# Second feed-forward projection with seven block products instead of eight, on 16 of its 22 blocks

## The chip, the cores and the metric

One core of a Trainium2 chip runs the whole kernel in one launch. The metric is the time of one execution on the device, in microseconds (us); lower is better. All inputs and the output lie in the chip's main memory as float32.

## The reference, cut to what matters

The reference is a stack of two layers with mixed attention and then two layers with a mixer and a convolutional feed-forward network (FFN). The change touches only the FFN, which runs twice (once in each of the last two layers), on S = 512 rows, a model width of 1024 and D_FF = 2816 inner units:

```python
def conv_ffn(x, w_up, conv_w, conv_b, w_down):
    a, g = jnp.split(x @ w_up, 2, axis=-1)
    g = lax.conv_general_dilated(g, conv_w[:, None, :].astype(g.dtype), window_strides=(1,),
                                 padding=((CONV_W - 1, 0),), dimension_numbers=('NWC', 'WIO', 'NWC'),
                                 feature_group_count=D_FF) + conv_b
    return (jax.nn.gelu(g) * a) @ w_down
...
    x = layer_norm(alpha * x + y, ln_g[l, 0], ln_b[l, 0])
    y = conv_ffn(x, ffn_w_up[l], ffn_conv_w[l], ffn_conv_b[l], ffn_w_down[l])
    x = layer_norm(alpha * x + y, ln_g[l, 1], ln_b[l, 1])
```

The second projection is a product of a 512 x 2816 matrix, gelu(g) * a, with w_down, 2816 x 1024. The inner units are cut into 22 blocks of 128.

## The kernel before, in words

**Numbers in two parts.** Each float32 operand of a large product is split into a rounded part `hi` (a cast on ACT) and a rest `lo` (a subtraction on DVE), and each product is three matmuls: hi·hi, hi·lo and lo·hi. `split` does this for activations, `load_w` for a weight tile: SP loads 128 x 512 float32 (256 KB) into one of four `raw` buffers (line 213), ACT writes `w[:, 0]` (line 226) and DVE writes `w[:, 1]` (line 227). `mm3` (lines 231 to 233) and `fsteps` (lines 1060 to 1062) issue the three matmuls. A weight tile `w` takes one of a set of slots, in turn: six that are always there (`NW`) and more that a stage adds with `more_w`. A slot comes free when the last matmul that reads it has run.

**The FFN (`ffn`, line 1467).** The hidden state stands transposed in `hT` (8 blocks of 128 x 512). The inner units are taken in three parts of 8, 7 and 7 blocks. In each part, groups of up to four blocks go through the first projection: eight weight tiles for `g`, and for each block j a pass of 8 steps of three matmuls (24 matmuls) into one PSUM bank, which `ev_g` reads (convolution on ACT and DVE, gelu on ACT); then eight weight tiles for `a`, with `ev_a`, which multiplies (line 1497) and splits the result into an `act` tile (lines 1499 and 1500). Then comes the second projection of the part: for each half n of the 1024 columns and each tile t of 128 rows, `down_part` runs one pass over the blocks of the part, three matmuls for each (`dsteps` and `mm3`), and adds the PSUM bank to `z[t]` on DVE (line 1532). With 8 blocks a part has 16 weight tiles, 8 passes of 24 matmuls and 8 additions to `z`. In the last part the layer norm follows each row tile (`ln_apply`), and in the first FFN the next layer's first loads are woven in.

The first group of an FFN runs in two halves of the rows (lines 1517 to 1519), since the last rows of `hT` come late. The FFN adds 7 slots for weight tiles to the 6 there are. Convolution weights are loaded into the tile `cwr` (lines 1475 and 1476), turned by TensorE (line 1506).

**What sets the order.** The program is unrolled. A scheduler fixes each engine's order when the kernel is built, from its own estimate of when each operand is ready; every engine and each DMA queue then runs its list in order and waits by semaphores. All DMAs are issued by SP. POOL (GpSimd) does small work only, in the FFN only the reciprocal root of the layer norm (lines 281 and 282). PSUM has eight banks: four for `mm`, two for `t` (transposes) and two for `o`, which the FFN doesn't use.

Of the kernel before, what the change touches and what calls it, by code (L numbers as in the profile page):

```python
# [9 lines left out]
F32 = mybir.dt.float32  # L10
F32R = mybir.dt.float32r
# [3 lines left out]
OP = mybir.AluOpType  # L15
# [5 lines left out]
S = 512  # L21
# [100 lines left out]
def _body(ctx, tc, nc, a, out, stop):  # L122
    V, SC, GP, PE = nc.vector, nc.scalar, nc.gpsimd, nc.tensor
# [30 lines left out]
    def ps_mm():  # L154
        return psum("mm", [128, 512], 4)
# [6 lines left out]
    def ps_o():  # L162
        return psum("o", [128, 512], 2)
# [34 lines left out]
    yT = hp.tile([128, 2, 4, S], F32R, name="yT")  # L198

    wslots = [(wp, NW)] * NW  # L200
    wturn = [0]

    def more_w(name, n, stack, side):
        pl = pool(name, stack=stack, side=side)
        wslots.extend([(pl, n)] * n)
        stack.callback(lambda: wslots.__delitem__(slice(len(wslots) - n, None)))
# [34 lines left out]
    def split(hi, lo, ps, scale=None):  # L241
        if scale is None:
            SC.copy(hi, ps)  # L243
            V.tensor_tensor(lo, ps, hi.bitcast(F32), op=OP.subtract)
        else:
            SC.activation(hi, ps, AF.Copy, scale=scale)
            V.scalar_tensor_tensor(lo, ps, scale, hi.bitcast(F32), op0=OP.mult, op1=OP.subtract)
# [64 lines left out]
    def tick():  # L312
        clock[0] += 1
        for p in [p for p in pend if p[0] <= clock[0]]:
            pend.remove(p)
            p[1]()
# [731 lines left out]
    R2 = math.sqrt(2.0)  # L1048
# [418 lines left out]
    def ffn(l, zst, z, rows, opf, est):  # L1467
        halves = (slice(0, 256), slice(256, 512))[::-1 if l else 1]
        fst = ExitStack()
        drain(opf)  # L1470
        est.close()
        fp = pool(f"ff{l}", stack=fst, side="left")
        more_w(f"wf{l}", 7, fst, "left")
        cwr = fp.tile([88, 128], F32, name="cwr")
        nc.sync.dma_start(cwr[0:66], a["ffn_conv_w_2"][l].rearrange("i (c p) -> (i c) p", p=128))
        nc.sync.dma_start(cwr[66:88], a["ffn_conv_b_2"][l].rearrange("(c p) -> c p", p=128))
        cw = fp.tile([128, 4, 22], F32, name="cw")
        up, down = a["ffn_w_up_2"][l], a["ffn_w_down_2"][l]
        c0 = 0
        st6 = {}  # L1480
        for part, nch in enumerate((8, 7, 7)):
            act = [fp.tile([128, 2, S], F32R, name="act", bufs=10) for _ in range(nch)]
            for q0 in range(0, nch, 4):
                nq = min(4, nch - q0)
                ge = {}

                def ev_g(j, ps):
                    c = c0 + q0 + j
                    g0 = fp.tile([128, S], F32, name="g0", bufs=2)
                    SC.activation(g0, ps, AF.Identity, scale=cw[:, 2, c:c + 1], bias=cw[:, 3, c:c + 1])  # L1490
                    V.scalar_tensor_tensor(g0[:, 1:], ps[:, :S - 1], cw[:, 1, c:c + 1], g0[:, 1:], op0=OP.mult, op1=OP.add)  # L1491
                    V.scalar_tensor_tensor(g0[:, 2:], ps[:, :S - 2], cw[:, 0, c:c + 1], g0[:, 2:], op0=OP.mult, op1=OP.add)
                    ge[j] = fp.tile([128, S], F32, name="ge", bufs=6)
                    SC.activation(ge[j], g0, AF.Gelu_apprx_tanh)

                def ev_a(j, ps):
                    V.tensor_tensor(ge[j], ge[j], ps, op=OP.mult)  # L1497
                    d = act[q0 + j]
                    SC.copy(d[:, 0], ge[j])
                    V.tensor_tensor(d[:, 1], ge[j], d[:, 0].bitcast(F32), op=OP.subtract)  # L1500

                ws = load_ws(up, FF + 128 * (c0 + q0), 128 * nq, K8)
# [45 lines left out]
                if m:  # L1548
                    save_x(t, z[t])

            if part == 2:
                lg = rows(1)
            w = [{k: load_w(down, 128 * (c0 + k), 512 * n, 512) for k in range(nch)} for n in range(2)]
            for t in (3, 2, 1, 0):
                down_part(0, w[0], t)
# [472 lines left out]
    zst, z, rows = z0[0]  # L2028
# [9 lines left out]
    zst, z, rows, opf, mst = odd_mixer()  # L2038
# [37 lines left out]
```

## Time and profile before

| | us |
|---|---|
| median of 3 runs | 1965.36 |
| lowest and highest | 1961.83, 1969.27 |
| the profiled execution, its own time | 1962.12 |
| its span, first to last instruction | 1960.3 |

PE (TensorE's matmuls) is busy for 97% of the span, DVE (VectorE) for 60%, ACT (ScalarE) for 40%, POOL for 10%. The two FFNs stand at about 894 to 1275 us and 1579 to 1957 us of the span. The page is read from the top: the engines' shares, then the chain that ended last, then the groups of instructions. Since matmuls overlap, the duration of one (0.39 us) is not what it costs; the distance between two starts is.

### The profile page before, as it was taken

What the parts mean: (1) busy time and instruction counts of PE and PEld (TensorE: products, weight loads), DVE (VectorE), ACT (ScalarE), POOL (GpSimd) and SP (SyncE); (2) the same over time, 40 slices, a digit from 0 to 9 for tenths busy, and PEclk for the clock granted to TensorE, in tenths of its full rate; (3) what the DMA queues carried; (4) which work ended last, traced back from release to release, by engine and by line L of the source; (5) the groups of instructions that cost most, each with busy time, mean ns of one, the idle gap of its engine ahead of it and who ended that gap; (6) DMA issues with size and microseconds to landing.
All of it is one profiled execution on the core that took longest, in us unless ns stands there. A gap on an engine that the chain in (4) does not pass through costs nothing.

```text
span 1960.3 us, 29102 instructions
## 1 busy us (share of the span) xinstructions
PE 1899.6 (97%) x10240; PEld 1540.1 (79%) x10240; DVE 1167.4 (60%) x2892; ACT 782.5 (40%) x1760; POOL 203.2 (10%) x316
## 2 busy tenths in 40 slices
PE   7999899999999999999999999999999999999998
PEld 4777687877888888768888888888778788888886
DVE  5698887475774235687434444645776774344445
ACT  2432454432553345444323333234665543233330
POOL 3011102012101000110000000101441200000001
PEclk9999999989999999999999999999999999999999
DMA  8535425135234233404322332352113042223321
GB/s 275 170 91 179 130 86 160 58 109 155 65 103 143 65 94 118 162 1 128 94 86 86 108 98 85 112 168 86 42 41 130 24 129 92 86 87 107 99 86 69
DMA packets 132872, 206.18 MB, mean 105 GB/s; under 512 B 20866, under 2 KB 57076, under 8 KB 132725
## 3 DMA queue, kind: packets, MB, share of 16 engines
q1 hardware_dynamic: 132724, 204.31, 33.9%
q8 instruction: 81, 1.33, 0.3%
q14 instruction: 67, 0.54, 0.1%
HBM read 194.62 MB, written 14.09 MB: 106 GB/s over the span
## 4 chain that ended last, share of the span: by engine, by line
PE 72%; DVE 6%; POOL 2%; DMA 1%; issue 1%; ACT 1%; POOLq 0%; DVEq 0%; ACTq 0%
PE mm L1060 11%; PE mm L1062 11%; PE mm L1061 11%; PE mm L231 9%; PE mm L233 9%; PE mm L232 8%; PE t L1095 1%; PE t L274 1%; PE o L1854 1%; PE o L1662 1%; PE mm L1924 1%; DVE w L227 1%; DVE z L1152 1%; DMA raw<-in_ffn_w_up_dram 1%; PE o L939 1%
## 5 line engine op out<-in xcount | busy, mean ns | idle before, releaser
L226 ACT CAST w<-raw 128x512 fp32r<-128x512 f32 (+4 forms) x568 | 321.8, 581 | 401.2 <-PE mm L233 172.1
L227 DVE TENSOR_TENSOR w<-raw,w 128x512 fp32r<-128x512 f32 (+4 forms) x560 | 348.4, 643 | 174.4 <-ACT w L226 171.7
L1060 PE MATMUL mm<-hT,w 128*128 128x512 f32 x920 | 367.0, 399 | 0.0
L1062 PE MATMUL mm<-hT,w 128*128 128x512 f32 x920 | 362.4, 394 | 0.0
L1061 PE MATMUL mm<-hT,w 128*128 128x512 f32 x920 | 361.6, 393 | 0.0
L231 PE MATMUL mm<-w,hT 128*128 128x512 f32 (+3 forms) x704 | 278.2, 396 | 1.2 <-ACT hT L243 1.2
L233 PE MATMUL mm<-w,hT 128*128 128x512 f32 (+3 forms) x704 | 263.2, 374 | 0.0
L232 PE MATMUL mm<-w,hT 128*128 128x512 f32 (+3 forms) x704 | 261.5, 371 | 0.5 <-DVE w L227 0.5
L1062 PEld LDWEIGHTS mm<-hT,w 128*128 128x128 f32 x920 | 172.6, 188 | 40.0 <-DVE w L227 0.8
L1060 PEld LDWEIGHTS mm<-hT,w 128*128 128x128 f32 x920 | 172.9, 188 | 39.7 <-ACT w L226 1.1
L1061 PEld LDWEIGHTS mm<-hT,w 128*128 128x128 f32 x920 | 172.9, 188 | 36.1
L231 PEld LDWEIGHTS mm<-w,hT 128*128 128x128 f32 x704 | 139.8, 199 | 30.4 <-issue 6.9
L233 PEld LDWEIGHTS mm<-w,hT 128*128 128x128 f32 x704 | 139.8, 199 | 20.7 <-issue 1.1
L232 PEld LDWEIGHTS mm<-w,hT 128*128 128x128 f32 x704 | 140.1, 199 | 16.8 <-issue 1.8
L231 PE MATMUL mm<-w,act 128*128 128x512 f32 x352 | 139.0, 395 | 0.0
L232 PE MATMUL mm<-w,act 128*128 128x512 f32 x352 | 138.3, 393 | 0.0
L233 PE MATMUL mm<-w,act 128*128 128x512 f32 x352 | 138.2, 393 | 0.0
L1532 DVE SCALAR_TENSOR_TENSOR z<-z,mm 128x512 f32<-128x512 f32 x48 | 33.0, 687 | 109.8 <-PE mm L233 109.8
L1491 DVE SCALAR_TENSOR_TENSOR g<-mm,cw,g 128x511 f32<-128x511 f32 x44 | 33.0, 749 | 100.2 <-ACT g L1490 100.2
L281 POOL TENSOR_SCALAR rp<-mv 128x1 f32<-128x1 f32 x16 | 9.8, 614 | 775.9 <-DVE mv L1146 774.9
L1090 ACT ACTIVATE E<-E,nm 128x128 f32<-128x128 f32 (+3 forms) x128 | 71.6, 560 | 45.5 <-DVE nm L1089 42.8
L1497 DVE TENSOR_TENSOR ge<-ge,mm 128x512 f32<-128x512 f32 x44 | 30.2, 686 | 83.3 <-PE mm L1062 83.3
(433 smaller groups left out, 3060.0 us busy)
## 6 DMA issues: line engine op xcount, KB each, us to landing
raw<-in_ffn_w_up_dram SPq DMA_DIRECT2D x128, 256.0 KB, 2.9
rawm<-in_w_mod_dram SPq DMA_DIRECT2D x96, 256.0 KB, 3.1
raw<-in_ffn_w_down_dram SPq DMA_DIRECT2D x88, 256.0 KB, 3.0
raw<-in_w_in_dram SPq DMA_DIRECT2D x80, 256.0 KB, 2.8
raw<-in_ev_w_in_dram SPq DMA_DIRECT2D x48, 256.0 KB, 3.1
raw<-in_ffn_w_up_dram SPq DMA_DIRECT2D x64, 192.0 KB, 2.4
raw<-in_w_out_dram SPq DMA_DIRECT2D x32, 256.0 KB, 3.0
raw<-in_w_in_dram SPq DMA_DIRECT2D x32, 128.0 KB, 3.5
```

What stands on the lines that cost most here:

```text
L226: SC.copy(hi, r)
L227: (eng or V).tensor_tensor(lo, r, hi.bitcast(F32), op=OP.subtract)
L231: PE.matmul(ps, hi, w[:, 0, w0:w0 + n], start=first, stop=False)
L232: PE.matmul(ps, hi, w[:, 1, w0:w0 + n], start=False, stop=False)
L233: PE.matmul(ps, lo, w[:, 0, w0:w0 + n], start=False, stop=last)
L1060: PE.matmul(ps, wh, hi, start=k == ks[0], stop=False)
L1061: PE.matmul(ps, wh, lo, start=False, stop=False)
L1062: PE.matmul(ps, wl, hi, start=False, stop=k == ks[-1])
L1090: SC.activation(E, E, AF.Exp, scale=scale, bias=nm, accum_out=den)
L1491: V.scalar_tensor_tensor(g0[:, 1:], ps[:, :S - 1], cw[:, 1, c:c + 1], g0[:, 1:], op0=OP.mult, op1=OP.add)
L1497: V.tensor_tensor(ge[j], ge[j], ps, op=OP.mult)
L1532: V.scalar_tensor_tensor(hs, hs, R2 if part == 0 else 1.0, ps, op0=OP.mult, op1=OP.add)
```

## The change

The parts have 8, 8 and 6 blocks. The first two are "quart" parts: their second projection is done by quarters. The blocks of a part go in pairs p = 0 to 3 (an even and an odd block), so that the activations are a 2 x 2 matrix of quarters (256 rows by even or odd block) and the weights are another (even or odd block by 512 columns). Seven products of sums of quarters (Strassen's scheme in a form with few sums) replace the eight products.

- `quarters` (called by `ev_a` at each odd block) forms the sums of activations of a pair on DVE and splits them: `k1`, `m`, `u2` of 512 columns and `v` of 256. Some of these tiles lie in `yT`, which is free then.
- `operand` makes the four weight tiles of one product. Three products start from a plain load by SP into a `bq` buffer (8 of them, 128 x 512); four add a further quarter of `w_down` to the buffer that is there by a DMA with `accum_op=add`, issued by POOL, and all seven split the buffer into a `w` tile. The buffers `y` take a plain load and three additions one after the other, `x` (which take over the buffers of `s`) a plain load and one addition.
- `product` runs 4 pairs x 2 row tiles x 3 matmuls into two PSUM banks (`W`, `X` or `Y`); `take` adds the bank to `z` or subtracts it. The banks `X` (of `o`) are kept over four products and read after each, `Y` over two. Each part has 14 such reads.
- The FFN adds 3 slots for weight tiles, not 7; `cwr` lies in a `g0` buffer, of which there are three, not two.

```diff
-        more_w(f"wf{l}", 7, fst, "left")
-        cwr = fp.tile([88, 128], F32, name="cwr")
+        more_w(f"wf{l}", 3, fst, "left")
+        cwr = fp.tile([128, S], F32, name="g0", bufs=3)[:88, :128]
...
-        for part, nch in enumerate((8, 7, 7)):
-            act = [fp.tile([128, 2, S], F32R, name="act", bufs=10) for _ in range(nch)]
+        for part, (nch, quart) in enumerate(((8, True), (8, True), (6, False))):
+            act, ops = [], {}
+            for c in range(nch):
+                if not quart:
+                    act.append(fp.tile([128, 2, S], F32R, name="act", bufs=10))
+                elif c % 2:
+                    kt = [yT[:, :, c // 2] if i == 0 and c < 4 else fp.tile([128, 2, S], F32R, name="act", bufs=10)
+                          for i in range(3)]
+                    kt.append(yT[:, :, 2 + c // 4, 256 * (c // 2 % 2):256 * (c // 2 % 2) + 256])
+                    ops[c // 2] = kt
+
+            def quarters(p, r0, r1):
+                lh, rh = slice(0, 256), slice(256, 512)
+                k1, m, u2, v = ops[p]
+                split(k1[:, 0], k1[:, 1], r1)
+                u = fp.tile([128, S], F32, name="g0", bufs=3)
+                V.tensor_tensor(u[:, lh], r0[:, lh], r0[:, rh], op=OP.subtract)
+                V.tensor_tensor(r0[:, rh], r1[:, rh], r0[:, rh], op=OP.subtract)
+                split(m[:, 0], m[:, 1], r0)
+                V.scalar_tensor_tensor(u[:, rh], r0[:, rh], -1.0, r0[:, lh], op0=OP.mult, op1=OP.subtract)
+                split(u2[:, 0], u2[:, 1], u)
+                V.scalar_tensor_tensor(r1[:, lh], u[:, rh], -1.0, r1[:, lh], op0=OP.mult, op1=OP.subtract)
+                split(v[:, 0], v[:, 1], r1[:, lh])
...
+                def operand(name, b, plus):
+                    ws = []
+                    for p in range(npair):
+                        if not plus:
+                            bufs[name, p] = fp.tile([128, 512], F32, name="bq", bufs=8)
+                            nc.sync.dma_start(bufs[name, p], src[b](p))
+                        else:
+                            GP.dma_start(bufs[name, p], src[b](p), accum_op=OP.add)
+                        wturn[0] = (wturn[0] + 1) % len(wslots)
+                        px, nx = wslots[wturn[0]]
+                        w = px.tile([128, 2, 512], F32R, tag="w", name="w", bufs=nx)
+                        split(w[:, 0], w[:, 1], bufs[name, p])
+                        ws.append(w)
+                    return ws
+
+                X = [ps_o() for _ in range(2)]
...
+                def take(n, t, sub, ps, mul=1.0):
+                    hs = z[t][:, 512 * n:512 * n + 512]
+                    V.scalar_tensor_tensor(hs, hs, mul, ps, op0=OP.mult, op1=OP.subtract if sub else OP.add)
+
+                def product(i, ws, bank, start, stop_, byr, evac):
+                    L = [lhs(i, r) for r in range(2)]
+                    for r, p in ([(r, p) for r in range(2) for p in range(npair)] if byr else
+                                 [(r, p) for p in range(npair) for r in range(2)]):
+                        if start and p == 0 and bank[r] is None:
+                            bank[r] = ps_mm()
...
+                o2 = operand("s", (1, 0), False)
+                o1 = operand("y", (0, 0), False)
+                product(1, o2, W, True, True, False, lambda r, ps: take(0, r, False, ps, first))
+                o5 = operand("y", (0, 1), True)
+                product(0, o1, X, True, False, False, lambda r, ps: take(0, r, False, ps))
+                o6 = operand("y", (1, 1), True)
+                product(4, o5, Y, True, False, False, lambda r, ps: take(1, 2 + r, True, ps, first))
+                o3 = operand("x", (1, 1), False)
+                product(5, o6, X, False, False, False, lambda r, ps: take(1, r, True, ps, first))
+                o7 = operand("x", (0, 1), True)
+                product(2, o3, Y, False, True, False, lambda r, ps: take(1, r, True, ps))
+                o4 = operand("y", (1, 0), True)
+                product(6, o7, X, False, False, True, lambda r, ps: take(1, 2 + r, True, ps))
+                product(3, o4, X, False, True, True, lambda r, ps: take(0, 2 + r, False, ps, first))
...
                 def ev_a(j, ps):
                     V.tensor_tensor(ge[j], ge[j], ps, op=OP.mult)
+                    if quart:
+                        if j % 2:
+                            quarters((q0 + j) // 2, ge[j - 1], ge[j])
+                        return
...
+            if quart:
+                down_quart()
+                c0 += nch
+                continue
+            lg = rows(1)
```

## Rows read from the trace of the kernel before

**Rows 1.** The page: busy time of each engine, and granted clock by slice.
```profile
PE 1899.6 (97%) x10240; PEld 1540.1 (79%) x10240; DVE 1167.4 (60%) x2892; ACT 782.5 (40%) x1760; POOL 203.2 (10%) x316
...
PEclk9999999989999999999999999999999999999999
```

**Rows 2.** Who waited for whom, PE alone, 906 to 1270 us: total, times, longest.
```profile
PE mm L1517 <- ACT w L226: 2.0, 1, 2.0
PE mm L232 <- DVE w L227: 0.5, 1, 0.5
```

**Rows 3.** Busy time by stretch: second projection of 8 blocks, then the next first projection.
```profile
core 0: us, PE busy (x) PEld busy (x) DVE busy (x) ACT busy (x) POOL busy (x), PEclk, DMA share, GB/s
...
994.00:1034.00 40.00, 40.00 (x175) 32.43 (x174) 13.01 (x20) 8.02 (x13) 0.00 (x0) 1.00 0.27 83
1034.00:1115.00 81.00, 81.00 (x353) 65.88 (x352) 40.33 (x65) 32.60 (x56) 0.00 (x0) 1.00 0.33 100
```

**Rows 4.** Timeline of DVE, second projection, 8 blocks: start, us, line, idle before.
```profile
1000.64 0.69 DVE L1532 SCALAR_TENSOR_TENSOR z<-z,mm 128x512 f32<-128x512 f32 x1 [4.90 <-PE mm L233]
1006.22 0.69 DVE L1532 SCALAR_TENSOR_TENSOR z<-z,mm 128x512 f32<-128x512 f32 x1 [4.90 <-PE mm L233]
...
1017.31 0.69 DVE L1532 SCALAR_TENSOR_TENSOR z<-z,mm 128x512 f32<-128x512 f32 x1 [1.69 <-PE mm L233]
1022.85 0.69 DVE L1532 SCALAR_TENSOR_TENSOR z<-z,mm 128x512 f32<-128x512 f32 x1 [4.85 <-PE mm L233]
```

**Rows 5.** Groups by line in 994 to 1034 us: busy, mean ns, idle before.
```profile
L232 PE MATMUL mm<-w,act 128*128 128x512 f32 x58 | 22.8, 394 | 0.0
...
L227 DVE TENSOR_TENSOR w<-raw,w 128x512 fp32r<-128x512 f32 x13 | 8.9, 692 | 4.7 <-ACT w L226 4.7
L226 ACT CAST w<-raw 128x512 fp32r<-128x512 f32 x13 | 8.0, 621 | 33.3 <-PE mm L233 31.6 <-DMA raw<-in_ffn_w_up_dram 1.1
L1532 DVE SCALAR_TENSOR_TENSOR z<-z,mm 128x512 f32<-128x512 f32 x7 | 4.8, 687 | 22.7 <-PE mm L233 22.7
```

**Rows 6.** Groups by line and shape, whole span, 256 columns: DVE, ACT.
```profile
L227 DVE TENSOR_TENSOR w<-raw,w 128x256 fp32r<-128x256 f32 x48 | 19.8, 432 | 23.9 <-ACT w L226 23.5
L536 DVE TENSOR_TENSOR qrot<-rot 128x256 f32<-128x256 f32 x16 | 6.0, 419 | 0.0
L226 ACT CAST w<-raw 128x256 fp32r<-128x256 f32 x48 | 18.8, 405 | 14.9 <-PE mm L233 8.9 <-DMA raw<-in_ev_w_in_dram 3.0 <-DMA raw<-in_w_in_dram 1.2
```

**Rows 7.** DMA: queues by kind (packets, MB, share), issues with median us to landing.
```profile
q1 hardware_dynamic: 132724, 204.31, 33.9%
q8 instruction: 81, 1.33, 0.3%
q14 instruction: 67, 0.54, 0.1%
...
raw<-in_ffn_w_down_dram SPq DMA_DIRECT2D x88, 256.0 KB, 3.0
...
z<-xd SPq DMA_DIRECT2D x8, 512.0 KB, 5.6
```

**Rows 8.** The tile z over the span: DMA to landing.
```profile
DMA to landing us min/median/max: 2.1/3.7/7.6
```

**Rows 9.** The tile raw in 900 to 1280 us: DMA to landing.
```profile
DMA to landing us min/median/max: 1.9/2.8/3.7
```

**Rows 10.** Who waited for whom, ACT alone, 906 to 1270 us: total, times, longest.
```profile
ACT w L226 <- PE mm L233: 71.1, 12, 14.4
ACT w L226 <- PE mm L1062: 35.9, 19, 4.9
...
ACT w L226 <- DMA raw<-in_ffn_w_up_dram: 21.1, 20, 4.6
```

**Rows 11.** Start of the FFNs: SP's waits 860 to 920 us; PE's wait in FFN 2.
```profile
SPq L1475 <- DVE hT L247: 55.1, 1, 55.1
...
PE mm L1517 <- ACT w L226: 2.6, 1, 2.6
```

More of the change, by code (lines that the diff above doesn't have):

```diff
@@ L1480, in ffn, with down_quart, lhs @@
         st6 = {}
-        for part, nch in enumerate((8, 7, 7)):
-            act = [fp.tile([128, 2, S], F32R, name="act", bufs=10) for _ in range(nch)]
+        for part, (nch, quart) in enumerate(((8, True), (8, True), (6, False))):
[20 more added lines that the diff above has]
+                split(v[:, 0], v[:, 1], r1[:, lh])
+            def down_quart():
+                npair = nch // 2
+                first = R2 if part == 0 else 1.0
+                src = {(i, n): lambda p, i=i, n=n: down[128 * (c0 + 2 * p + i):128 * (c0 + 2 * p + i) + 128, 512 * n:512 * n + 512]
+                       for i in range(2) for n in range(2)}
+                bufs = {}
+                def operand(name, b, plus):
[13 more added lines that the diff above has]
+                X = [ps_o() for _ in range(2)]
+                W, Y = [None] * 2, [None] * 2
+                def lhs(i, r):
+                    t, o = ((1, 0), (0, 0), (3, 0), (0, 256), (1, 256), (2, 256), (2, 0))[i]
+                    return [ops[p][t][:, :, o + 128 * r:o + 128 * r + 128] for p in range(npair)]
+                def take(n, t, sub, ps, mul=1.0):
[7 more added lines that the diff above has]
+                            bank[r] = ps_mm()
+                        tick()
+                        h, ps, w = L[r][p], bank[r], ws[p]
+                        PE.matmul(ps, h[:, 0], w[:, 0], start=start and p == 0, stop=False, skip_group_check=True)
+                        PE.matmul(ps, h[:, 0], w[:, 1], start=False, stop=False, skip_group_check=True)
+                        PE.matmul(ps, h[:, 1], w[:, 0], start=False, stop=stop_ and p == npair - 1, skip_group_check=True)
+                        if p == npair - 1:
+                            evac(r, ps)
+                o2 = operand("s", (1, 0), False)
[12 more added lines that the diff above has]
+                product(3, o4, X, False, True, True, lambda r, ps: take(0, 2 + r, False, ps, first))
@@ L1488, in ev_g @@
                     c = c0 + q0 + j
-                    g0 = fp.tile([128, S], F32, name="g0", bufs=2)
+                    g0 = fp.tile([128, S], F32, name="g0", bufs=3)
                     SC.activation(g0, ps, AF.Identity, scale=cw[:, 2, c:c + 1], bias=cw[:, 3, c:c + 1])
@@ L1549, in finish @@
                     save_x(t, z[t])
-            if part == 2:
-                lg = rows(1)
+            if quart:
[3 more added lines that the diff above has]
+            lg = rows(1)
             w = [{k: load_w(down, 128 * (c0 + k), 512 * n, 512) for k in range(nch)} for n in range(2)]
```

## The prediction

> **What bounds the kernel now.** I read the page first: PE is busy for 97% of the span at the upper one of its two clock levels (2.4 GHz) in nearly every slice, DVE for 60%, ACT for 40% [rows 1]. Busy time alone doesn't tell that an engine sets the end, so the second view is who waits for whom in the FFN: in 364 us of the first FFN PE waits twice, 2.5 us together [rows 2]. Third, the stretches: in the second projection of an 8-block part PE is busy 40.0 of 40 us, DVE 13.0, ACT 8.0, and in the next first projection PE 81.0 of 81, DVE 40.3 [rows 3]. So in the FFN the end is set by the number of matmuls, and a matmul taken out is worth its pitch, as long as nothing new makes PE wait.
>
> What the pitch is can't be read from the duration: 394 ns each [rows 5], but they overlap. The DVE timeline gives it: `z` is added to once for each pass of 24 matmuls, at 1000.64 and 1006.22 us and at 1017.31 and 1022.85 [rows 4], so a pass takes 5.58 and 5.54 us, 5.56 in the mean, or 0.232 us for a matmul.
>
> **What is removed.** Part sizes don't change the count for a block: before, a block costs 4 x 2 passes x 3 = 24 matmuls, and 16 blocks 384. Now each of two quart parts has seven products of 4 pairs x 2 row tiles x 3 = 24 matmuls, 168 in a part and 336 for the 16 blocks. That is 48 for an FFN, 96 in all, or four passes: 4 x 5.56 = **22.2 us less on PE**. (By the duration it would be 96 x 0.394 = 37.8 us, too much by the overlap.) The first projection and the last part keep their matmuls per block.
>
> The Trainium skill (Trainium Kernel Development and Optimization, Performance Expectations) says that busy time of matmuls is a poor measure since they are pipelined, and prefers the busy share of weight loads. By that rule PE in this stretch would have idle time to sell, 32.4 of 40 us [rows 3], and by that share (0.81) the four passes would be worth 18.0 us instead of 22.2; the row of waits shows no such idle time, and I keep the pitch.
>
> **What is added, on DVE and ACT.** A quart part splits 28 weight tiles instead of 16: 12 more at 0.69 us on DVE and 0.62 on ACT [rows 5], 8.3 and 7.4 us. It reads PSUM 14 times instead of 8: 6 x 0.69 = 4.1 us. `quarters` has, for a pair, three splits of 512 columns and one of 256, and four sums of 256: on DVE 3 x 0.69 + 0.43 + 4 x 0.42 = 4.2 us, on ACT 3 x 0.62 + 0.41 = 2.3 [rows 5, 6], in place of two splits (1.4 and 1.2): 4 x 2.8 = 11.2 and 4 x 1.1 = 4.3. In all 23.6 us on DVE and 11.7 on ACT for a part, 94 and 47 us for four. None of it is on the path by sum: a part lasts some 120 us and DVE has 41 of 81 us free above it in the first projection [rows 3].
>
> It is tight only in the second projection. There 7 x 5.56 = 38.9 us of PE stand against, on DVE, 28 splits (19.3), 14 reads (9.6), the product and the quarters of the last pair (0.7 + 4.2) and the 8 splits for the next group (5.5), 39.3 us, less the 8 splits of the first two operands, which can be done during the last pass before (5.5): 33.8 of 38.9, 5.1 us to spare. Cover holds, but thinly; before it was 13.0 of 40.
>
> **What is added, transfers.** Plain loads fall from 16 to 12 for a part; 16 adding DMAs come, on POOL's queue. The trace of before has no DMA from POOL and none that adds [rows 7], so the time L from issue to landing has to be bounded. Below: a plain load of the same 256 KB, 3.0 us [rows 7]. Above: an adding DMA also reads and writes the old 256 KB; the nearest rows are `z`, 512 KB, 5.6 us in the median and 7.6 at most [rows 7, 8]. Even that is no proof, since none of them adds. I take 5, nearer to the double-size row than to the plain one.
>
> The Trainium skill (DMA: Bandwidth & Descriptors, Anatomy of one DMA) prices a DMA from GpSimd at about 2.0 us plus its bytes at 436 GB/s; the estimate for 256 KB is 2.6 us, for a plain one, and with it the sum below stays as it is. No run here shows one yet.
>
> What L has to fit: count from the start D of the first product. The last pass of the first projection frees its eight weight slots 0.69 us apart from D - 5.56 on; the spare ninth and the first three go to `o2`, the fourth to seventh to `o1`. So `o1` gets its first slot at D - 2.8, and is split by D - 1.4 (0.62 + 0.69). Then `y` goes through addition, split, addition, split: `o6` is ready at D - 1.4 + 2 x (L + 1.3), and is wanted for the fourth product at D + 16.7. It fits if L is up to 7.7; `o5`, wanted at D + 11.1, fits up to 11.2. The fourth pair comes later by about 3 us in split and is wanted later by 4.2. `o7` and `o4` have more room: for `o4` the buffer is there by D + 16.2 at L = 5 (D - 1.4 + 12.6 + 5), and it is wanted at D + 33.4. POOL's queue carries the 16 in order; it must do one in 2.4 us (38.9 / 16), and nothing else stands on it in these parts (busy 0 in both stretches [rows 3]). With L = 5: **no cost**, 0 to 0 between the bounds 3.0 and 7.6, and more only above.
>
> **What is moved: fewer slots.** Nine instead of thirteen. ACT's casts wait on PE's release of slots already, 71.1 + 35.9 us, and for raw loads 21.1 [rows 10]; neither reaches PE. With nine, a new group of eight tiles has one tile ahead of it; tile k follows the release of slot k - 1 in the last pass, at 0.69 k, plus 1.3 us of split, and is wanted 5.56 us after that. Tiles 5 to 7 also wait for a raw buffer: split of tile k - 4 (0.69 (k - 4) + 1.3), landing 2.8 us [rows 9], split 1.3; tile 5 at 6.1 us against 9.0. Slack is 2.8 us, 1.9 with the longest landing of 3.7. Where a group ends with `quarters`, its 4.9 us on DVE fall into that gap if the list puts them first: up to 1.5 us lost, at one place in each quart part. I take 1.5 us in all, of 0 to 6. For the last part's groups of two blocks tiles are half as wide and the last pass as long; no cost.
>
> **What is moved: the start of an FFN.** `cwr` takes other memory and the first eight tiles have 9 slots. SP waited 55.1 us there for the memory of `cwr`, with raw loads behind it, and PE waited 2.0 and 2.6 us for casts [rows 2, 11]. The new place can take away these waits (-2 each) or lengthen them by a landing (+3 each); I take +1 each, **2 us**.
>
> **Sum.** 1962.1 (the profiled execution's own time, 1.8 above its span) - 22.2 + 1.5 + 2 = 1943.4. The median of before is 3.2 us above its profiled execution; half of that is added, **1945 us**, 1.0% less than 1965.4. Differences under about 0.5% (9.8 us) can't be told from no change with this kernel; faster therefore means below 1955.5 and slower above 1975.2.
>
> **Rivals.**
> *The addition chain decides (slower).* If L is over 7.7 us, PE waits for `o6` in each part for 2 x (L - 7.7). The gain of 5.56 for a part is gone at L = 10.5; the time is slower by 0.5% from L = 11.7, and at L = 13 the wait is 10.6 x 4 = 42 us, 1987 us with the rest of the sum. Against it: every row of twice the bytes lands within 7.6. For it: L is not shown at all, four additions queue on one engine, each waits for both splits, and casts of later operands stand behind a late one in ACT's and DVE's lists. A mechanism for so long an L here: descriptors that POOL writes could be held up by DVE, which would be busy for 33.8 of 38.9 us. The Trainium skill (SBUF — State Buffer, Who interferes with whom) has such a rule, that GpSimd can't write descriptors while DVE holds their common port, though its own list leaves out `tensor_tensor`, most of DVE's work here; no run here shows it yet. Chance 0.17.
>
> *Slots and raw loads become late at every change of group.* 24 changes in two FFNs, each losing one step of three matmuls (0.69 us) as tiles come one step late: 16.7 us more than nothing, so 1945 - 1.5 + 16.7 = 1960 us, no change. For: slots bound ACT already [rows 10]. Against: 2.8 us of slack by the sum above. Chance 0.14.
>
> *DVE becomes the bound of the second projection.* DVE waits for ACT's cast before each weight split, 4.7 us for 13 [rows 5], 0.36 each. If 28 such gaps can't be filled, 10.1 us stand against 5.1 to spare, 5 x 4 = 20 us: 1965, no change. Chance 0.06.
>
> **How the numbers follow.** Forecast 0.63, at 1945 (1937 to 1953); chain 0.17 (0.15 of it slower, 0.02 within); slots 0.14 (0.03 of it still faster, 0.11 within); DVE 0.06 within. Faster 0.66, within 0.5% 0.19, slower 0.15. The range starts at 1937 (starts at -2 each instead of +1, group ends at 0, about 7.5 less) and reaches to 1970 over the two middle cases; the chain's slow cases are left out, with a little below.
>
> **What would show it.** Right: PE's matmuls of the second projection fall from 1056 to 960; a pitch of 5.56 us between the reads of a product's end; PE's waits in the FFN still a few us; DVE's busy time up by about 94 us to 1262 and ACT's by 47 to 829; casts of adding operands done before their product. Wrong: PE waiting for the cast or rest of `o6`, the fourth product (L over 7.7 in the DMA view), waits of PE at a group's first steps after `quarters` (slots), DVE without gaps in the second projection, or a longer pitch of matmuls.

## The result and the profile after

| | us |
|---|---|
| median of the changed kernel, 14 runs | 1975.06 (1967.31 to 1986.17) |
| median of before beside it, 14 runs | 1963.93 |
| ratio, 95% interval | 1.006 [1.004, 1.008] |
| profiled execution, its time and its span | 1974.4, 1972.6 |

The changed kernel is slower by 0.6%, where 1945 us, 1% faster, was predicted. By the profiled executions the difference is 12.3 us.

The page answers [rows 1 and 7]: busy time, granted clock by slice, the DMA queues (packets, MB, share of 16 engines), and the shares of the chain that ended last, by line.

```profile
PE 1891.2 (96%) x10144; PEld 1530.2 (78%) x10144; DVE 1250.6 (63%) x3060; ACT 825.2 (42%) x1840; POOL 259.9 (13%) x380
...
PEclk9989999999999999999999999999999999999999
...
q1 hardware_dynamic: 130420, 200.11, 32.9%
q0 software_dynamic: 9216, 16.78, 5.5%
...
PE mm L1060 6%; PE mm L1062 6%; PE mm L1061 6%; DMA bq<-in_ffn_w_down_dram 6%; PE mm L231 5%; PE mm L233 5%; PE mm L232 5%; PE t L1095 1%; PE t L274 1%; POOL bq L1519 1%; DVE w L227 1%; PE o L1945 1%; PE o L1753 1%; DVE z L1152 1%; PE o L939 1%
```

The 96 matmuls are gone (10240 to 10144), and PE is busy for 8.4 us less, yet the span is 12.3 us longer. A queue that was not there, q0, moves 16.78 MB, and `DMA bq<-in_ffn_w_down_dram` has 6% of the chain.

Who waited for whom, PE alone, 860 to 1290 us (total, times, longest), answers [rows 2]:

```profile
PE o L1546 <- DVE z L1536: 9.4, 2, 5.1
PE mm L1546 <- DVE z L1536: 2.5, 2, 1.6
PE mm L1546 <- ACT act L243: 1.8, 2, 1.6
```

Line 1546 is the first matmul of a step in `product`, line 1536 is `take`. Before, the longest wait here was 2.0 us; now two last 9.4 us together, one in each quart part, at `o`, where the sixth product in order (that of `o7`) goes on in the bank of the fourth. The stretches of the first second projection, 985 to 1034 us, answer [rows 3]:

```profile
core 0: us, PE busy (x) PEld busy (x) DVE busy (x) ACT busy (x) POOL busy (x), PEclk, DMA share, GB/s
985.00:1016.00 31.00, 28.84 (x121) 22.02 (x120) 17.36 (x30) 10.51 (x19) 14.29 (x16) 1.00 0.82 135
1016.00:1021.00 5.00, 1.17 (x6) 0.63 (x4) 2.66 (x5) 2.86 (x6) 0.00 (x0) 1.00 0.91 218
1021.00:1025.00 4.00, 3.54 (x10) 2.86 (x11) 4.00 (x8) 1.59 (x4) 0.00 (x0) 0.57 0.57 189
1025.00:1034.00 9.00, 9.00 (x40) 7.31 (x39) 6.99 (x11) 4.22 (x7) 0.00 (x0) 1.00 0.73 226
```

PE stands from 1016.8 to 1021.5 us. Then the granted clock is 0.57, near the lower level (1.2 of 2.4 GHz), and PE makes 10 matmuls in 4 us, where the pitch of [rows 4] would give 17. So the wait is paid and then part of it once more.

**Where the 12.3 us come from.** From the first matmul of a second projection to the first of the next stage, the four quart parts take 48.1, 50.3, 46.8 and 48.9 us: 38.5 us more than 4 x 38.9 at full pitch. 19.6 of these are the waits at the sixth product (each with the matmul that ends it), 3.9 the waits at the fifth, 4.4 those in the first for the last pair's `k1`, 8.0 slow matmuls after the long waits (0.43 us from start to start instead of 0.23), and the other 2.6 small gaps. The starts of the two FFNs became 3.5 and 1.1 us shorter. So -22.2 + 38.5 - 4.6 = +11.7, and 0.6 is left over.

**The chain itself.** The chain of work in the first of these stretches (start, us, what), from the additions of `o5` to the start of the sixth product:

```profile
986.39 0.72 POOL bq L1519
987.11 7.71 DMA bq<-in_ffn_w_down_dram
...
994.92 0.62 ACT w L243
995.54 0.32 ACT yT L243
...
995.87 0.25 DVE yT L244
...
996.22 0.68 DVE z L1536
996.90 0.24 DVE w L244
...
997.42 0.70 DVE w L244
...
998.63 6.91 DMA bq<-in_ffn_w_down_dram
...
1008.62 2.41 POOL bq L1519 x4
1011.03 8.25 DMA bq<-in_ffn_w_down_dram
...
1019.37 0.63 ACT w L243
...
1020.63 0.47 DVE z L1536
```

Three adding DMAs stand in a row: one of `o5` (lands at 994.82), one of `o6` (1005.54), one of `o7` (1019.27). In this order of lists `o3`'s splits stand behind those of `o6`, and `o7`'s additions wait for `o3`'s splits. In POOL's list they also stand behind the four additions for `o4`, which is wanted last. Between `o5` and `o6` the cast and rest of the last pair's `v` (`yT`) and a read of PSUM come first, 3.3 us. And the landings take 7 to 8 us, not 5.

What ends PE's wait is a read: the sixth product goes on in the bank of the fourth, and may start only after `take` has read it (1020.63). The fourth product had ended by 1010, but its read stands behind `o7`'s four splits in DVE's list, and DVE idles ahead of the first of them. The first of these splits and the read:

```profile
1015.60 0.69 DVE L244 TENSOR_TENSOR w<-bq,w 128x512 fp32r<-128x512 f32 x1 [3.68 <-ACT w L243]
...
1020.63 1.28 DVE L1536 SCALAR_TENSOR_TENSOR z<-z,o 128x512 f32<-128x512 f32 x2
```

An estimate from these rows: with the read in that gap PE would have found the tiles of `o7` ready at 1016.3, 1018.0, 1019.4 and 1020.7, and would have waited some 1.6 us in place of 4.5. So the late additions set the time, and the place of one read in a list makes more of it. No run moved that read alone. The waits at the fifth product end in the same way, with a read behind `o3`'s splits.

### The profile page after: what moved, and what is told of

Its sections match the earlier page's. It is cut to its first block, busy times and chain, and to the rows that moved or that the text cites. A ratio compares the mean times of both kernels' runs of the same rounds, so it can differ in the third digit from the quotient of the medians.

```text
span 1972.6 us, 29313 instructions
## 1 busy us (share of the span) xinstructions
PE 1891.2 (96%) x10144; PEld 1530.2 (78%) x10144; DVE 1250.6 (63%) x3060; ACT 825.2 (42%) x1840; POOL 259.9 (13%) x380
## 3 DMA queue, kind: packets, MB, share of 16 engines
q0 software_dynamic: 9216, 16.78, 5.5%
## 4 chain that ended last, share of the span: by engine, by line
PE 49%; issue 17%; DMA 7%; DVE 7%; POOL 3%; ACT 2%; SPq 0%; POOLq 0%; DVEq 0%; ACTq 0%
PE mm L1060 6%; PE mm L1062 6%; PE mm L1061 6%; DMA bq<-in_ffn_w_down_dram 6%; PE mm L231 5%; PE mm L233 5%; PE mm L232 5%; PE t L1095 1%; PE t L274 1%; POOL bq L1519 1%; DVE w L227 1%; PE o L1945 1%; PE o L1753 1%; DVE z L1152 1%; PE o L939 1%
## 5 line engine op out<-in xcount | busy, mean ns | idle before, releaser
L227 DVE TENSOR_TENSOR w<-raw,w 128x512 fp32r<-128x512 f32 (+4 forms) x496 | 308.5, 641 | 140.8 <-ACT w L226 138.7
L226 ACT CAST w<-raw 128x512 fp32r<-128x512 f32 (+4 forms) x504 | 284.6, 576 | 248.7 <-PE mm L233 54.8
L231 PEld LDWEIGHTS mm<-w,hT 128*128 128x128 f32 x704 | 141.2, 201 | 30.4 <-issue 6.2
L233 PEld LDWEIGHTS mm<-w,hT 128*128 128x128 f32 x704 | 141.4, 201 | 21.9 <-DVE hT L244 1.3
L232 PEld LDWEIGHTS mm<-w,hT 128*128 128x128 f32 x704 | 141.7, 201 | 16.6 <-issue 1.8
L1519 POOL DMA_DIRECT2D bq<-in_ffn_w_down_dram x64 | 56.6, 1229 | 444.6 <-DVE w L244 440.3
L244 DVE TENSOR_TENSOR w<-bq,w 128x512 fp32r<-128x512 f32 x112 | 73.8, 689 | 57.9 <-ACT w L243 57.6
L243 ACT CAST w<-bq 128x512 fp32r<-128x512 f32 x112 | 66.3, 619 | 99.6 <-DMA bq<-in_ffn_w_down_dram 83.0
L1574 ACT ACTIVATE g<-mm,cw 128x512 f32<-128x512 f32 x44 | 34.2, 778 | 79.8 <-PE mm L1062 63.4
L1085 DVE COPY pT<-t 128x512 f32<-128x512 f32 (+3 forms) x84 | 43.1, 513 | 37.5 <-PE t L1280 22.9
```

The lines of the kernel that those rows point to most:

```text
L226: SC.copy(hi, r)
L227: (eng or V).tensor_tensor(lo, r, hi.bitcast(F32), op=OP.subtract)
L231: PE.matmul(ps, hi, w[:, 0, w0:w0 + n], start=first, stop=False)
L232: PE.matmul(ps, hi, w[:, 1, w0:w0 + n], start=False, stop=False)
L233: PE.matmul(ps, lo, w[:, 0, w0:w0 + n], start=False, stop=last)
L1519: GP.dma_start(bufs[name, p], src[b](p), accum_op=OP.add)
```

## The experiments

Where an experiment alters the second projection, its "excess" is the sum over the four quart parts of their length above 38.9 us; the changed kernel has 38.5.

### Is it the adding DMAs at all

`e2_no_chain`: every operand is loaded plainly by SP into a buffer of its own.

```diff
-                            GP.dma_start(bufs[name, p], src[b](p), accum_op=OP.add)
+                            bufs[name, p] = fp.tile([128, 512], F32, name="bq", bufs=8)
+                            nc.sync.dma_start(bufs[name, p], src[b](p))
```

> The changed kernel with every operand loaded plainly by SP into a buffer of its own turn; the additions are left out of the computation, and nothing waits for an earlier operand's split but the turn of the buffers. Matmuls, splits, reads of PSUM, slots are as in the changed kernel. If the chain of additions is the whole loss of 38 us, the waits of PE in the second projections all but vanish and the time is 1975 - 38 = 1937 us (1933 to 1945). If DVE's thin margin or the nine slots share in it, PE still loses more than 3 us in a part, and the time stays above 1950.

Measured 1935.47 us, ratio 0.9873 [0.9836, 0.9909], excess -0.2. Its span, 1933.5 us, is that of before (1960.3) less 22.2 for the matmuls and 4.6 for the starts. That it fits so closely is partly luck, since the four runs of e2 lie between 1932.5 and 1947.3 us. The whole 38.5 us hang on how the sums of weights are formed; splits, reads, `quarters` and the nine slots cost nothing.

`e1_pool_no_add`: the same DMAs from POOL, behind the same waits, but each overwrites the buffer.

```diff
-                            GP.dma_start(bufs[name, p], src[b](p), accum_op=OP.add)
+                            GP.dma_start(bufs[name, p], src[b](p))
```

> The changed kernel with the additions left out: the 16 DMAs of a part that add are still issued by POOL, into the same buffers and behind the same waits, but overwrite them (the sums of weights are left out of the computation). It tells adding from the queue. In the changed kernel these DMAs land 6.2 us after issue (median) and PE loses 38 us in four second projections. If adding makes them slow, they land in about 3 us, as a plain load did before, three landings in a row are 9 us shorter, and the loss falls to under 10 us: about 1945 us. If being issued and described by POOL makes them slow, they still land in about 6 us and the time stays at 1970 to 1980.

Measured 1939.34 us, ratio 0.9887 [0.9858, 0.9917], excess 1.6. The four issues of `o5` in the first quart part, first in the changed kernel, then in e1 (ns on POOL; us from issue to landing):

```profile
L1519 POOL DMA_DIRECT2D bq<-in_ffn_w_down_dram x4: 1082/1344/1677, 985.0 to 987.1; - x4
DMA to landing us min/median/max: 4.1/6.4/7.7
```

```profile
L1519 POOL DMA_DIRECT2D bq<-in_ffn_w_down_dram x4: 536/542/779, 985.5 to 987.6; - x4
DMA to landing us min/median/max: 3.7/3.8/3.9
```

And e1's queue of POOL, beside q0 above:

```profile
q0 software_dynamic: 5120, 16.78, 2.6%
```

The chain with its three landings in a row is all there in e1, and it fits, since a landing takes 2.7 to 4.5 us in the whole run, 3.8 in the median, and hardly more when four are queued. With the addition the first of four lands after 4.1 us, but the others after 5.7, 7.1 and 7.7. The same 16.78 MB take 5.5% of the DMA engines instead of 2.6%.

### Is it the order of the operands

`e3_x_first`: `o3` is loaded and split ahead of the additions of `o6`, and `o7`'s additions are put ahead of the product of `o6`.

```diff
+                o3 = operand("x", (1, 1), False)
                 o6 = operand("y", (1, 1), True)
                 product(4, o5, Y, True, False, False, lambda r, ps: take(1, 2 + r, True, ps, first))
-                o3 = operand("x", (1, 1), False)
+                o7 = operand("x", (0, 1), True)
                 product(5, o6, X, False, False, False, lambda r, ps: take(1, r, True, ps, first))
                 product(2, o3, Y, False, True, False, lambda r, ps: take(1, r, True, ps))
-                o7 = operand("x", (0, 1), True)
```

> The changed kernel, same work, with the operand o3 formed ahead of o6 and o7 ahead of the product of o6, so that its split doesn't stand behind the late o6 in the lists of ACT and DVE. If the order of these lists puts three landings in a row (o5, o6, o7), the wait for o7 (19.6 us in four parts) and most of the slow clock after it (9 us) go: 1975 - 25 = 1950 us. If the landing time of each adding DMA or POOL's queue is the bound, another operand becomes as late, and the time stays within 5 us of 1975.

Measured 1957.58 us, ratio 0.9974 [0.9956, 0.9991], excess 20.3: half of the loss goes with nothing but another order. The time lies between the two that were expected (1950, and 1970 to 1980). PE's wait at the sixth product is still there, 3.0 us in the first part, and the landings are longer, since POOL now issues nine in a row. POOL's row, and the first two casts on ACT after those of `o6`:

```profile
1000.26 7.98 POOL L1519 DMA_DIRECT2D bq<-in_ffn_w_down_dram  x9 [5.37 <-DVE w L244]
```

```profile
1010.38 0.62 ACT L243 CAST w<-bq 128x512 fp32r<-128x512 f32 x1 [0.66 <-DMA bq<-in_ffn_w_down_dram]
1015.51 0.62 ACT L243 CAST w<-bq 128x512 fp32r<-128x512 f32 x1 [4.51 <-DMA bq<-in_ffn_w_down_dram]
```

But it is not `o7` that is late there. Its four additions land from 1010.28 to 1014.13, and PE comes to the sixth product at 1017.7. The cast at 1010.38 is the first of `o7`; the one at 1015.51 waits for the first addition of `o4`. The scheduler put the four casts of `o4` ahead of the other three of `o7`, and the read of the fourth product on DVE (1020.08) behind three of `o4`'s splits. So this wait, too, is one of list order behind late additions.

Two more runs cut one link each. `e9_o7_plain` loads `o7`'s block plainly into a fresh buffer, `e10_o6_plain` that of `o6`:

```diff
-                        if not plus:
+                        if not plus or plus == 2:
...
-                o7 = operand("x", (0, 1), True)
+                o7 = operand("x", (0, 1), 2)
```

> The changed kernel, but the block of o7 is loaded plainly by SP into a fresh buffer instead of being added to o3's: the sum of o7 is left out, so that o7 no longer stands behind the additions of o5 and o6. Theory (three landings in a row, o5, o6 and, behind o3's splits in the lists of ACT and DVE, o7, cost the time; two in a row fit): the 4 to 6 us wait of PE at the sixth product and the slow stretch after it go in every quart part, some 29 of the 38 us; left are the waits at the third and fourth products, 5 to 9 us. About 1945 us (1938 to 1950). The prediction's own count (two landings in a row for o6, which fits up to 7.7 us) gives the same for what is left. Rival (every adding transfer that is too long costs by itself, whatever stands behind it): 48 of 64 adding transfers remain, so three quarters of the 38 us, some 28, remain: about 1965 us.

> The changed kernel, but the block of o6 is loaded plainly by SP into a fresh buffer instead of being added to o5's sum (o6 and o4 are left with a part of their sums). o7 is still added to o3's buffer after o3's splits. Theory (three landings in a row): the middle one is gone, o3's splits and so the additions of o7 come earlier by an addition of 6 to 8 us, more than the 4 to 6 us that PE waits at the sixth product; what stays is at most the wait for the weight slots and last quarters at the third product, up to 5 us in all: about 1940 us (1936 to 1948). Rival (the additions of o7 are late for a reason of their own, the queue of POOL or the number of them, and not for what they stand behind): PE's wait at the sixth product stays, some 29 of 38 us: about 1965 us.

Measured 1960.08 us, ratio 0.9969 [0.9952, 0.9985], excess 18.6 for e9; 1952.62, ratio 0.9924 [0.9899, 0.995], excess 14.4 for e10. Both lie between the theory (1945, 1940) and the rival (1965): "three landings of a fixed length" is not the whole reason. (The waits that were to stay, named there at the third and fourth products, stand at the first and the fifth in e9, at the first in e10.) In e10 the rest shows at the sixth product, where PE waits longest (2.3 us in the first part). First POOL's list, then ACT's casts of `o7`:

```profile
988.10 3.76 POOL L1519 DMA_DIRECT2D bq<-in_ffn_w_down_dram  x4 [86.75 <-DVE w L244]
1001.91 7.14 POOL L1519 DMA_DIRECT2D bq<-in_ffn_w_down_dram  x8 [10.05 <-DVE w L244]
```

```profile
1013.94 0.62 ACT L243 CAST w<-bq 128x512 fp32r<-128x512 f32 x1 [7.99 <-DMA bq<-in_ffn_w_down_dram]
1015.27 0.62 ACT L243 CAST w<-bq 128x512 fp32r<-128x512 f32 x1 [0.71 <-DMA bq<-in_ffn_w_down_dram]
1016.53 0.62 ACT L243 CAST w<-bq 128x512 fp32r<-128x512 f32 x1 [0.64 <-DMA bq<-in_ffn_w_down_dram]
1017.77 2.70 ACT L243 CAST w<-bq 128x512 fp32r<-128x512 f32 x5 [0.62 <-DMA bq<-in_ffn_w_down_dram]
```

The eight start between 1001.91 and 1007.32, and land 4.3, 7.6, 8.2, 8.8, 8.3, 9.1, 9.7 and 10.4 us after their issue; from the second on they come 1.2 to 1.3 us apart, the distance of the casts above. The first cast of `o3` there starts at 1001.13 and its rest can't be done before 1002.4, so the addition issued at 1001.91 is none of `o7`'s: additions for `o4`, which nobody needs yet, are ahead of those for `o7`. The queue finishes one addition behind the other. In e9 a wait of 1.2 to 2.1 us is left in each part too; there the read of the fourth product stands behind splits that wait for weight slots, and how much of the 18.6 us is due to the buffers that the fresh loads of `o7` take was not separated.

### What the time of an addition goes with

The same 64 adding DMAs with half the bytes: `e11_half_columns` adds 256 of 512 columns (as many rows), `e12_half_rows` 64 of 128 partitions (half the rows).

```diff
-                            GP.dma_start(bufs[name, p], src[b](p), accum_op=OP.add)
+                            GP.dma_start(bufs[name, p][:, :256], src[b](p)[:, :256], accum_op=OP.add)
```

> The changed kernel with the same 64 adding DMAs, each over 256 of the 512 columns (128 rows of 1 KB instead of 2 KB): half of every added block is left out of the sums. In the changed kernel an adding DMA that is issued alone lands in 4.0 to 4.2 us, and one in a burst of four in 4.1, 5.7, 7.1 and 7.7 us after its issue, with landings 1.3 to 2.4 us apart; the plain ones from POOL's queue land in 3.7 to 3.9 us, all four. Theory (the queue does additions one behind the other, and the time of one goes with its bytes): landings in a burst come 0.6 to 1.2 us apart, the fourth lands 4 to 5.5 us after its issue, most of PE's waits and slow stretches go: 1937 to 1948 us. Rival (one behind the other, but the time goes with the number of rows or of DMAs): landings and time as in the changed kernel, 7 to 8 us for the fourth and 1970 to 1980 us.

> The changed kernel with the same 64 adding DMAs, each over 64 of the 128 partitions (64 rows of 2 KB): half of every added block is left out of the sums. The bytes of a DMA are those of the run with half the columns, the rows are half as many. If the time of an addition goes with its bytes, both runs give the same, 1937 to 1948 us with the fourth landing of a burst after 4 to 5.5 us; if it goes with its rows, only this one does, and the other stays at 1970 to 1980 us; if it goes with the number of DMAs, both stay there. A third possibility would be seen here alone: that 64 partitions use fewer of the DMA engines, and take as long as 128, which would leave this one slow beside a fast one with half the columns.

Measured 1938.36 us, ratio 0.9848 [0.9816, 0.988], excess 0.8; and 1943.21, ratio 0.9876 [0.9848, 0.9904], excess 0.9. The same four issues of `o5`, e11 and then e12:

```profile
L1519 POOL DMA_DIRECT2D bq<-in_ffn_w_down_dram x4: 1082/1348/1677, 989.6 to 991.6; - x4
DMA to landing us min/median/max: 3.6/4.0/4.3
```

```profile
L1519 POOL DMA_DIRECT2D bq<-in_ffn_w_down_dram x4: 1070/1272/1503, 988.9 to 991.0; - x4
DMA to landing us min/median/max: 3.6/4.1/4.6
```

With 128 KB each the landing hardly grows in a burst, and the loss is gone, though what waits for what, the number of additions and POOL's time for an issue are those of the changed kernel. So it was not POOL's list (1348 ns in e11 as 1344 in the changed kernel), nor the number of DMAs, nor that of their packets (e11's queue has as many as q0 above), nor the chain by itself:

```profile
q0 software_dynamic: 9216, 8.39, 3.0%
```

It was the time that the queue takes for 256 KB added, in lists that leave room for about 5 us a landing. That room is an estimate by the chain above: PE came to the sixth product 4.7 us before it could start, and 3.1 us late by earlier waits; three landings took 22.9 us, so each may take (22.9 - 4.7 - 3.1) / 3 = 5.0 us. Whether the queue itself sets the pace, or the DMA engines that it shares with SP's loads (busy for 82 and 91% in the first two stretches above), was not separated.

### The sums formed elsewhere

`e8_dve_adds`: SP loads the further quarter into a `raw` buffer, DVE adds. `e6_pool_adds` is the same with `GP.tensor_tensor`.

```diff
-                            GP.dma_start(bufs[name, p], src[b](p), accum_op=OP.add)
+                            t = wp.tile([128, 512], F32, tag="raw", name="raw", bufs=4)
+                            nc.sync.dma_start(t, src[b](p))
+                            V.tensor_tensor(bufs[name, p], bufs[name, p], t, op=OP.add)
```

> The changed kernel with the sums formed by DVE: the addend is loaded plainly by SP into a raw buffer and DVE adds it (16 more operations of 0.69 us, 11.0 us for a part). By the sum of the prediction DVE had 33.8 of 38.9 us to do in a second projection, so it becomes the bound: 44.8 us, 5.9 us over, 4 x 5.9 = 24 us, 1961 us. If part of this work lies ahead in the first projection, it is less, 1940 to 1950.

> The changed kernel with the same sums, formed otherwise: the addend is loaded plainly by SP into one of the four raw buffers and POOL adds it to the buffer (128 x 512, about 1.3 us, as POOL's rows of 1.28 us in the kernel before). The chain stays, with 1.3 us in place of 6.2 for a link. If the time of a link is the cause, the waits go and the time is 1937 to 1945 us. If POOL's additions and DVE hold each other up (28 splits and 16 additions in 39 us), DVE's subtractions grow beyond 0.69 us and PE still waits: above 1955 us.

**e8 measured 1940.45 us, ratio 0.9885 [0.9864, 0.9906]: it beats both kernels**, the one before by 1.1%. Excess -0.2, as without any sums. The second projections of its four quart parts, busy time of PE, PEld, DVE, ACT, POOL:

```profile
988.00:1026.00 38.00, 38.00 (x167) 30.93 (x166) 36.81 (x62) 16.38 (x29) 0.00 (x0) 1.00 0.54 184
1115.00:1153.00 38.00, 38.00 (x165) 30.78 (x165) 36.65 (x62) 16.70 (x29) 0.00 (x0) 1.00 0.39 125
1661.00:1699.50 38.50, 38.50 (x167) 31.13 (x166) 36.97 (x63) 16.45 (x29) 0.00 (x0) 1.00 0.54 185
1788.00:1826.50 38.50, 38.50 (x169) 31.36 (x168) 37.40 (x64) 17.60 (x31) 0.00 (x0) 1.00 0.43 135
```

DVE is busy for 96 to 97% of these stretches, with 16 additions more for a part, and still PE doesn't wait once. So the expected bound (44.8 us of DVE, 1961 us) did not come. The time is in the other expected range, 1940 to 1950, but not for its reason: in the first part only one of the 16 additions ran ahead of the second projection. What was wrong is the price. Operations on DVE overlap a little, and where they follow each other three take 1.89 us:

```profile
999.56 1.89 DVE L1521 TENSOR_TENSOR bq<-bq,raw 128x512 f32<-128x512 f32 x3
```

That is 0.60 us from start to start for a duration of 0.69. At this price 44.8 us become an estimate of 39.0, which just fits into 38.9. The sum of two values that are on the chip costs 0.60 us on an engine that has just room for it; as an addition by DMA it takes 4 to 8 us on the path.

e6 measured 1959.24 us, ratio 0.9984 [0.9968, 0.9999], excess 21.8. Groups by line in e6, the last a POOL row of the same form elsewhere in it:

```profile
L244 DVE TENSOR_TENSOR w<-bq,w 128x512 fp32r<-128x512 f32 x112 | 116.8, 1083 | 1.4 <-ACT w L243 0.8
L1521 POOL TENSOR_TENSOR bq<-bq,raw 128x512 f32<-128x512 f32 x64 | 107.1, 1704 | 403.5 <-DVE w L244 403.5
...
L227 POOL TENSOR_TENSOR w<-raw,w 128x512 fp32r<-128x512 f32 x8 | 10.5, 1338 | 1.4 <-ACT w L226 1.4
```

The same DVE subtraction takes 1083 ns beside POOL's additions, 689 in the changed kernel, and POOL's takes 1704 where others take 1338: the two hold each other up. The Trainium skill (SBUF — State Buffer, Who interferes with whom) says so: a DVE instruction with two inputs from SBUF contends with a GpSimd instruction that reads SBUF. These rows agree.

`e7b_dram_sums`: all 64 sums are formed ahead in the chip's main memory (a copy and an adding DMA each, from POOL's queue), and the operands are plain loads.

```diff
+                GP.dma_start(sums[l, c0, p, o], q(c0, p, *b))
+                GP.dma_start(sums[l, c0, p, o], x, accum_op=OP.add)
...
-                            GP.dma_start(bufs[name, p], src[b](p), accum_op=OP.add)
+                            bufs[name, p] = fp.tile([128, 512], F32, name="bq", bufs=8)
+                            nc.sync.dma_start(bufs[name, p], sums[l, c0, p, plus])
```

> The changed kernel with the sums of weights formed ahead in main memory: POOL's DMAs copy the quarters and add to them, for the first FFN while the mixer ahead of it runs, for the second during the first; the second projection then loads each operand plainly by SP. The 64 adding DMAs are all there, but no operand waits for one in the second projection. If their place in the chain is the cause and not their number, the time is that of the kernel without a chain, 1937 to 1945 us. If their traffic or POOL's blocked list holds up the mixer, the gain is eaten there: above 1950 us, with the second projections at 39 us each.

Measured 2021.95 us, ratio 1.03 [1.0277, 1.0323]. The excess is -0.2, but the scheduler put all the copies and additions of both FFNs at the kernel's start. The page's slices, PE, granted clock, DMA:

```profile
PE   3558999999999999999999999999999999999997
...
PEclk7788699999999999999999999999999999999999
DMA  9999644332521523340335333335214033432422
```

With the DMA engines full in the first four slices PE is busy for 3 to 8 tenths of them, and the first FFN starts 91 us later than in e2. It doesn't tell what the sums would cost if they were spread over stretches with idle DMA engines; that was not tried.

### The starts of the FFNs

The kernel before with 3 slots instead of 7 (`e4_before_3_slots`), and with `cwr` in a `g0` buffer (`e5_before_cwr`):

```diff
-        more_w(f"wf{l}", 7, fst, "left")
+        more_w(f"wf{l}", 3, fst, "left")
```

```diff
-        cwr = fp.tile([88, 128], F32, name="cwr")
+        cwr = fp.tile([128, S], F32, name="g0", bufs=3)[:88, :128]
```

> The kernel before with 3 added slots for weight tiles in the FFN instead of 7, nothing else. If nine slots suffice, as the sum of the prediction has it (slack 2.8 us at a change of group), PE's waits stay as they are and the time is within 5 us of the kernel before, 1964. If slots become late at every change of group, it is 10 to 17 us slower, 1974 to 1981.

> The kernel before with cwr in one of three g0 buffers, as in the change, nothing else. In the changed kernel the first group of the two FFNs ends 3.5 and 1.1 us earlier than before. If the memory of cwr is the reason, this kernel is 3 to 5 us faster than the kernel before; if the fewer slots or the other memory plan are, it is the same within 2 us.

Measured 1958.67 us, ratio 0.9982 [0.9968, 0.9997] for e4, and 1964.73, ratio 1.0003 [0.9987, 1.002] for e5. In e4 the two starts (first matmul of the FFN to the first of its second group) take 24.5 and 27.7 us; before 28.4 and 29.0, in e5 28.5 and 28.8, in the changed kernel 24.9 and 27.9. So it is the fewer slots, not `cwr`, that shorten the starts, and nine slots cost nothing elsewhere. Why four slots less help there was not traced further; one reading, argued only, is that the memory of the added slots is free earlier.

## Why the prediction was wrong

**Held: the 22.2 us.** e2 and e8 have their second projections at 38.7 to 39.0 us each, seven passes of 5.56, without a gap. The pitch from DVE's timeline [rows 4] was the right price.

**Held: DVE and ACT, with DVE priced too high.** 1262 and 829 us were predicted, 1250.6 and 825.2 came. DVE's growth is 83 us where 94 were predicted: the number of operations was right (168 more), but the prediction took durations, 0.69 us, where operations that follow each other cost 0.60. It had avoided just this mistake for PE. The cover that was judged "thinly" was therefore wider, and in e8 16 additions more for a part fit into it without a wait of PE. That rival (DVE the bound, 0.06) is out even at 97%.

**Failed: "no cost, 0 to 0 between the bounds 3.0 and 7.6".** This is the step that turned the sign, 38.5 us against 0.
- *L was taken as one number.* For an adding DMA that finds the queue idle 5 us was about right: 3.8 to 5.5. But `operand` issues four at once, and within a burst the queue finishes 256 KB only every 1.2 to 3.9 us, so the fourth lands after 7.2 to 7.7, and after up to 9.1 where other additions are ahead of it (10.4 in e10). The prediction asked of the queue one in 2.4 us in the mean, and stopped there; a mean says nothing of the last of a burst.
- *"`o7` and `o4` have more room."* The sum followed the buffers: `x` takes one addition, `y` three. It did not follow the lists. `o3` needs no addition, but its splits stand behind those of `o6` on ACT and DVE, so `o7`'s additions follow `o6`'s landing, a third one in the same row, and in POOL's list they follow those of `o4`. Reads of PSUM stand behind the late splits on DVE, and PE's long wait ends with such a read, at the sixth product, not at the fourth, where the prediction would have looked for it. e3 shows what the lists are worth: with others, and even longer landings, half the loss goes.
- *The price of a wait.* The prediction put 2 us for each us of L too much. Here a 4 to 6 us wait comes with a stretch of slow matmuls after it (granted clock 0.57 in the one shown), and 8.0 of the 38.5 us are these matmuls, not waits.

**The rival that came true.** "The addition chain decides" had the right mechanism and 0.17. Its threshold, 7.7 us at `o6`, was about right for `o6`: with landings of 7.7 and 6.9 us the fourth product waits no more than 0.5 us. But it was not the one that binds: that is at `o7`, behind a third landing, where the room is nearer to 5. The sentence that casts of later operands stand behind a late one in the lists was named there, as a risk, and not put into the sum. What it offered as the cause of a long L, DVE holding up the descriptors that POOL writes, is not what happened: POOL's issue time is the same in e11, where the loss is gone, and e1's plain DMAs land in 3.8 us beside the same DVE work. The Trainium skill (DMA: Bandwidth & Descriptors, Anatomy of one DMA) led to an estimate of 2.6 us for a plain one; e1's shortest is 2.7, its median 3.8. What an addition costs more is not in that formula.

**Wrong in sign, small: slots and starts.** +1.5 and +2 were put in (the 1.5 doesn't follow from the 4.9 and 2.8 us beside it, which leave 2.1), -4.6 came (e4: nine slots alone make the kernel before 2.4 us faster by the medians). The rival of slots late at each change of group is out: e4 and e2 have no such gaps.

So the range (1937 to 1970) missed by 5 us, on the side of the rival whose slow cases were left out of it.

## What to carry to other kernels

- Price a new transfer as it will be issued: four at once on one queue need the time of the last, not of one. And follow a chain through each engine's list, not only through the buffers: an operand that needs nothing stands behind one that waits.
- An adding DMA saves an engine's 0.6 us and puts 4 to 8 us on the path; where the sum is needed within a few passes and an engine has the room by the trace, let the engine add (e8).
- Ask of each engine what it costs from start to start, not how long one operation lasts: 0.232 us against 0.39 for a matmul, 0.60 against 0.69 on DVE.
- A wait of 4 us on PE cost more than 4 us here: the four long waits of the changed kernel, 19.6 us, were followed by 8.0 us lost to slow matmuls.

## What was not expected of the hardware

- An adding DMA of 256 KB that found the queue idle landed in 3.8 to 5.5 us, near a plain one from the same queue (2.7 to 4.5), but in a row they finished 1.2 to 3.9 us apart, though issued 0.5 to 0.8 us apart, and took twice the share of the DMA engines for the same bytes (5.5% against 2.6%).
- The issue of an adding DMA lasts 0.85 to 2.0 us on POOL by its rows, that of a plain one 0.54; half the bytes in as many rows doesn't shorten it (1348 ns against 1344). But these rows overlap: in a burst the next issue starts 0.5 to 0.8 us later with either kind.
- After more than 4 us of waiting PE ran at a granted clock of 0.57 for the next 4 us.
- Operations of 0.69 us on DVE started 0.60 us apart where nothing held them up (e8).
